# Forming and splitting the feed-forward's gated products in PSUM instead of SBUF

## The chip, the cores and the metric

The kernel runs on one core of a Trainium2 chip. The metric is the device time of one execution in microseconds (us); the median of several runs counts. Engines: TensorE (PE), VectorE (DVE), ScalarE (ACT), GpSimd (POOL), and the DMA queue that SyncE (SP) issues.

## What is computed

Two layers of a hybrid backbone over 512 latent and 256 context tokens of width 1024. Each layer mixes the tokens (Fourier mixing, retention, neighbourhood attention), then applies a gated feed-forward of inner width 2816. The change touches only the feed-forward:

```python
D_FF = ((8 * D_MODEL // 3 + 255) // 256) * 256        # 2816

def swiglu(h, w1, w3, w2):
    return (jax.nn.silu(h @ w1) * (h @ w3)) @ w2

# in each layer
#   x = x + gate * swiglu(rmsnorm(x) modulated, w1, w3, w2)
```

The last layer computes the latent tokens alone.

## The kernel before

**Split operands.** Every matmul operand is kept as two float32r parts: a high part (a ScalarE cast of the fp32 value) and a low part (value minus high part, a subtraction on VectorE or GpSimd). A product is three matmuls: high by high, low by high, high by low (`mm3`, L398 to L400).

**Jobs of seven products.** The products with w1 and w3 are done by Strassen's scheme in Winograd's form. A job is a pair of chunks of 128 output features (r = 0 and 1) for the two halves of the tokens (c = 0 and 1). Its products are issued in the order P1, P2, P6, P7, P4, P5, P3. Each is 12 matmuls of n columns into one PSUM bank, n = 384 in layer 0 and 256 in layer 1. `complete` takes each bank in: P1 is copied to a sum U by ScalarE (L1591); P6 and P7 are added to sums by VectorE (L1595, L1598); P2, P4, P5 and P3 complete the blocks (r, c) = (0, 0), (1, 0), (1, 1) and (0, 1) in `block`. After P5, U also takes the product in for P3 (L1603).

**A block.** For w1, VectorE adds bank and U into the gate tile (L1629) and ScalarE applies SiLU (L1630). For w3, VectorE adds bank and U into a temporary `t` (L1633) and multiplies `t` by the gate into a temporary `g` (L1634); `put` then casts the high part on ScalarE (L1460) and subtracts for the low part (L1461), on VectorE for r = 0 and on GpSimd for r = 1. There are 11 w3 jobs with four blocks in each layer, 44 blocks of n = 384 and 44 of n = 256.

**Parts and the products with w2.** Layer 0 has parts of 2, 1, 2, 2, 2, 2 pairs of jobs (w1, w3), layer 1 of 2, 2, 2, 2, 1, 2. After each part but the last, `plain` multiplies the part's gated products by w2 and VectorE adds the result to the residual x (L1657). The first token half (in layer 0 the first 512 tokens) comes first, for two output chunks together; the gated products of the part's last job come last in each chunk. In this document a handoff is the place where `plain` or `finish` begins to read the part's gated products.

**Weights.** A weight unit arrives by DMA; VectorE forms the sums that Strassen's scheme needs (L225 S, L226, L227, L229); ScalarE casts the high part (L183) and GpSimd, for a few VectorE, subtracts the low part (L188). In layer 0 VectorE also does the next layer's modulation (L522) beside the feed-forward; ScalarE's part of it is L517.

**Order.** The program is scheduled by hand: every engine executes its instructions in the order in which the program writes them, and waits in place. PSUM has eight banks of 512 fp32 columns (`ps`), given out in the order in which they come free; a bank is free when its last reader is done. The first part of each layer begins differently: P1 and P2 of all its four jobs are issued together, beside the layer norm, so that four banks hold P2 until the job's P6 has come. The text calls this the start of a layer's feed-forward.

Of the kernel before, what the change touches and what calls it, by code (L numbers as in the profile page):

```python
# [27 lines left out]
# feed-forward: pairs of chunks between two returns to the residual stream, by layer  # L28
# [5 lines left out]
# for each layer, where the parts of the attentions lie beside the projections: times after the ends of some;  # L34
# the four heads' retention, the readout, the three pairs' of heads neighbourhoods, the first values
# [5 lines left out]
# steps of the operands' preparation beside the first products  # L41
PREP = (0, 1, 1, 2), (1, 1, 1, 2)
# products of the two-by-two scheme in the order of their use
# half of the latent tokens, in the order of the columns, whose mirror images are the others
# [5 lines left out]
# columns of the vector blob  # L50
V_C, V_BADA, V_GMIX, V_GFFN, V_GFIN, V_RETG, V_DEC, V_SEL, V_RP, V_END = 0, 16, 112, 128, 144, 152, 158, 174, 176, 178
# columns of the constant blob
C_ID, C_BLK, C_END = 0, 128, 256
# columns of the decay strips: latent tiles, edge tile, context-context, context-latent
# [4 lines left out]
class Job:  # L59
    """a pair of chunks of outputs, from pairs of chunks of inputs and for two halves of the tokens, by seven  # L60
    products (Strassen's scheme in Winograd's form):
    P1 = A11 B11, P2 = A12 B21, P3 = S4 B22, P4 = A22 T4, P5 = S1 T1, P6 = S2 T2, P7 = S3 T3,
    S1 = A21 + A22, S2 = S1 - A11, S3 = A11 - A21, S4 = A12 - S2,
    T1 = B12 - B11, T2 = B22 - T1, T3 = B22 - B12, T4 = B21 - T2;
    C11 = P1 + P2, C12 = P1 + P6 + P5 + P3, C22 = P1 + P6 + P7 + P5, C21 = P1 + P6 + P7 + P4"""

# [6 lines left out]
def in_order(jobs, after, window):  # L73
    """the order of the jobs' steps on the tensor engine: the oldest job's first step whose operands are there;
    after[key, step]: pairs of another step and a delay"""
    end, t, out = {}, 0.0, []
# [25 lines left out]
class WeightStream:  # L102
    """DMA of the weights in the order of their use, running ahead, and their split into two float32r parts."""

    SLOTS = 11
    # the units of a job that the weights of a product are made from
    USES = {1: (0,), 2: (0,), 3: (0,), 4: (1,), 5: (), 6: (0, 1), 7: (0, 1)}

    def __init__(self, kern, raws, parts):
        self.k = kern  # L110
        self.max_raws, self.max_parts = raws, parts
        self.units, self.tasks = [], []
        self.raw, self.parts, self.size, self.pending = {}, {}, {}, []
        self.when = {}
        self.n_dma = self.n_split = self.n_raw = self.n_parts = 0
        self.limit = 10**6
        # products whose weights' second parts are the vector engine's, of the first jobs and the others
        self.lead, self.dve = {}, {}
        # parts that may go to other places, and those that are there
        self.spare, self.away = 0, set()  # L120
# [5 lines left out]
    def add_step(self, job, p, aps):  # L126
        """the weights of one product of a job, from the two units of its outputs"""
# [8 lines left out]
    def issue(self):  # L136
        """start loads while there is room"""
        k = self.k
# [27 lines left out]
    def part(self, n):  # L166
        """tiles for the two parts of n columns"""
# [23 lines left out]
    def split(self):  # L191
        """split the next unit, or put it aside for its callback"""
# [18 lines left out]
    def form(self, job, p):  # L211
        """the sums that the weights of product p are made from, and those after it"""
# [9 lines left out]
        if p == 6:  # L222
            # S2 takes the place of A11, S3 that of A21 and S4 that of A12
# [49 lines left out]
    def get(self, key):  # L273
        """the parts of a unit, to be followed by done() after its last use"""
        self.flush()
        self.pump()
        return self.parts.pop(key)
# [7 lines left out]
def beside(first, second, kern):  # L285
    """Run two generators side by side; each yields the tensor-engine time of what it has just emitted,
    which kern.pe adds up. The second also yields spans (from, to, cost): its next work lies between these
    times of the first."""
# [22 lines left out]
def pieces(st):  # L311
    """the latent and the context tokens of a stream: which, columns of all tokens, columns of the stream"""
# [7 lines left out]
class Norm:  # L320
    """a layer norm done step by step: the sums, the rows' factors, then a chunk at a time"""
# [28 lines left out]
class Kern:  # L350
# [10 lines left out]
    # ---- tiles  # L361
    def table(self, key, ap):
        """a table of 1024 columns, loaded ahead of its use"""
# [30 lines left out]
    # ---- products of split operands  # L394
    def mm3(self, out, a, b, start, stop):
        """out += a^T b for a = (hi, lo), b = (hi, lo) without the product of the two low parts"""
# [9 lines left out]
    # ---- set-up  # L406
# [18 lines left out]
    def decay_logs(self):  # L425
        """log_sigmoid of the decay logits: min(x, 0) - 2 atanh(z), z = e / (2 + e), e = exp(-|x|)"""
# [21 lines left out]
    # ---- adaLN modulation  # L448
    def ada_load(self, k):
        """weights of the first layer's first shift and scale for the features 8 p + k"""  # L450
# [9 lines left out]
    def ada_first(self, k):  # L460
        """the two's modulation of the features 8 p + k: four groups of columns of the tensor engine share
        the sums, the rows of one stream are then added and turned to partitions"""
# [39 lines left out]
    def ada_unit(self, layer, part, i):  # L502
        """a unit of the first layer's parts in use before its feed-forward, for the tensor engine;
        of the others, for the vector engine"""
# [7 lines left out]
    def silu_tables(self):  # L512
        """silu of the two conditions on all partitions"""
# [5 lines left out]
    def ada_dve(self, raw, layer, part, i):  # L519
        """modulation of the features 8 p + i: a row's products with the condition, summed"""  # L520
# [69 lines left out]
    # ---- layer norm with modulation  # L590
    def sumsq(self, x, m, acc, st):
        """add the squares of chunk m of the residual stream to the sums of acc, those of the last chunk beside them"""
# [8 lines left out]
    def rstd(self, acc, n, merge=True):  # L601
        """1 / RMS of the n tokens, on all partitions of a bank: roots and reciprocals are taken with
        the tokens on partitions"""
# [18 lines left out]
    def modulate(self, x, rs, st, layer, f, h):  # L622
        """h = x rstd g (1 + sc) + sh, split; a generator over the chunks"""
# [37 lines left out]
    # ---- projections  # L661
    def proj(self, key, h, streams, evac):
        """features on partitions: a chunk of 128 columns of the weight against the streams"""
# [18 lines left out]
    def proj_v(self, keys, h, out, norms=None, late=1, heads=False):  # L682
        """tokens on partitions: 384 columns of the weight for the six token tiles;
        with norms the latent tiles come first, beside the layer norms of the two streams"""
# [27 lines left out]
        if heads:  # L712
            # for each token tile the heads' parts side by side, the second of two heads with its low part first
# [17 lines left out]
    def evac_rope(self, dst, tab):  # L731
        """rotary embedding of the latent tokens; the pairs lie 16 partitions apart"""
# [18 lines left out]
    # ---- retention  # L751
    def strip_piece(self, layer, h, piece, delta, st):
        """decay factors of one piece of the strips, an engine's work at a time: delta holds its distances,
        st takes them"""
# [4 lines left out]
        if piece == "cx":  # L759
            # from the context's state in either direction  # L760
# [13 lines left out]
        # both directions have the diagonal  # L774
# [9 lines left out]
    def pieces(self, work):  # L784
        """strip pieces (layer, head, piece, delta, st), a step behind one another"""
# [16 lines left out]
    def strips_first(self):  # L802
        """the first layer's strips: the first head's stay, the others' go to DRAM"""
# [3 lines left out]
        # the distances  # L807
# [43 lines left out]
    def strips_ahead(self, layer, heads):  # L851
        """strips of a later layer, kept in DRAM"""
# [1393 lines left out]
```

## Time and profile before

| what | value |
|---|---|
| runs of the kernel | 1754.65, 1755.63, 1760.47 us, median 1755.63 |
| span of the profiled execution | 1759.0 us |
| PE busy | 1655.9 us, 94% of the span |
| DVE busy | 1219.6 us, 69% |
| POOL busy | 867.1 us, 49% |
| ACT busy | 744.6 us, 42% |
| mean granted TensorE clock | 0.978 |

The profile is of one execution, from its first to its last instruction; no separate time of that execution is listed, so its span stands for it. Busy times add up the durations of an engine's instructions. The layer-0 feed-forward lies between about 480 and 1000 us, that of layer 1 between about 1370 and 1759 us.

### The profile page before, as it was taken

What the parts mean: (1) busy time and instruction counts of PE and PEld (TensorE: products, weight loads), DVE (VectorE), ACT (ScalarE), POOL (GpSimd) and SP (SyncE); (2) the same over time, 40 slices, a digit from 0 to 9 for tenths busy, and PEclk for the clock granted to TensorE, in tenths of its full rate; (3) what the DMA queues carried; (4) which work ended last, traced back from release to release, by engine and by line L of the source; (5) the groups of instructions that cost most, each with busy time, mean ns of one, the idle gap of its engine ahead of it and who ended that gap; (6) DMA issues with size and microseconds to landing.
All of it is one profiled execution on the core that took longest, in us unless ns stands there. A gap on an engine that the chain in (4) does not pass through costs nothing. (4 is left out here: it accounts for less than half of the span.)

```text
span 1759.0 us, 26982 instructions
## 1 busy us (share of the span) xinstructions
PE 1655.9 (94%) x10054; PEld 1481.4 (84%) x10054; DVE 1219.6 (69%) x2040; ACT 744.6 (42%) x1437; POOL 867.1 (49%) x621
## 2 busy tenths in 40 slices
PE   6989999999979998999999999999998799999997
PEld 4867777778978987798999997778788799999997
DVE  6866555664687899586776867764656877767585
ACT  5544434454453223232332554444554444334333
POOL 3343231022467557465665833532035787677673
PEclk9999999999989999999999999999999899999998
DMA  9354243244122343434343444422132232332222
GB/s 344 131 193 133 71 148 94 91 135 167 37 72 85 110 142 108 132 120 132 124 153 114 135 164 138 141 71 87 61 120 73 66 103 87 95 109 84 64 94 72
DMA packets 76387, 202.33 MB, mean 115 GB/s; under 512 B 12704, under 2 KB 19488, under 8 KB 75872
## 3 DMA queue, kind: packets, MB, share of 16 engines
q1 hardware_dynamic: 76256, 200.60, 35.0%
q8 instruction: 80, 1.31, 0.3%
q14 instruction: 51, 0.42, 0.1%
HBM read 184.25 MB, written 11.80 MB: 111 GB/s over the span
## 5 line engine op out<-in xcount | busy, mean ns | idle before, releaser
L188 POOL TENSOR_TENSOR wp<-wr,wp 128x512 fp32r<-128x512 f32 (+1 forms) x336 | 477.5, 1433 | 275.4 <-ACT wp L183 271.8
L399 PE MATMUL f<-hp,wp 128*128 128x384 f32 (+1 forms) x1232 | 387.7, 315 | 13.9 <-POOL wp L188 7.6
L398 PE MATMUL f<-hp,wp 128*128 128x384 f32 (+1 forms) x1232 | 386.9, 314 | 14.5 <-DVE U L1598 5.3
L400 PE MATMUL f<-hp,wp 128*128 128x384 f32 (+1 forms) x1232 | 386.0, 313 | 3.9 <-POOL hp L1523 3.5
L183 ACT CAST wp<-wr 128x512 fp32r<-128x512 f32 (+1 forms) x360 | 213.0, 607 | 355.1 <-PE f L400 117.0
L188 POOL TENSOR_TENSOR wl<-wr,wh 128x1024 fp32r<-128x1024 f32 (+2 forms) x75 | 163.7, 2187 | 379.4 <-ACT wh L183 251.1
L399 PEld LDWEIGHTS f<-hp,wp 128*128 128x128 f32 x1232 | 238.3, 193 | 19.6 <-POOL wp L188 12.9
L398 PEld LDWEIGHTS f<-hp,wp 128*128 128x128 f32 x1232 | 238.6, 194 | 17.8 <-issue 9.7
L400 PEld LDWEIGHTS f<-hp,wp 128*128 128x128 f32 x1232 | 238.4, 194 | 5.2 <-POOL hp L1523 4.3
L398 PE MATMUL f<-g,wp 128*128 128x256 f32 (+1 forms) x576 | 183.6, 319 | 12.8 <-ACT g L1460 12.6
L400 PE MATMUL f<-g,wp 128*128 128x256 f32 (+1 forms) x576 | 183.3, 318 | 4.8 <-POOL g L1461 4.2
L399 PE MATMUL f<-g,wp 128*128 128x256 f32 (+1 forms) x576 | 182.4, 317 | 0.0
L398 PE MATMUL proj<-h,wh 128*128 128x512 f32 (+1 forms) x456 | 167.7, 368 | 0.9 <-DVE v L404 0.9
L399 PE MATMUL proj<-h,wl 128*128 128x512 f32 (+1 forms) x456 | 159.4, 350 | 0.7 <-POOL wl L188 0.7
L400 PE MATMUL proj<-h,wh 128*128 128x512 f32 (+1 forms) x456 | 159.1, 349 | 0.0
L1657 DVE SCALAR_TENSOR_TENSOR x<-f,mod,x 128x256 f32<-128x256 f32 (+1 forms) x160 | 83.8, 546 | 82.8 <-PE f L400 82.7
L398 PEld LDWEIGHTS f<-g,wp 128*128 128x128 f32 x576 | 113.2, 197 | 21.8 <-ACT g L1460 15.2
L400 PEld LDWEIGHTS f<-g,wp 128*128 128x128 f32 x576 | 113.0, 196 | 13.6 <-POOL g L1461 4.8
L399 PEld LDWEIGHTS f<-g,wp 128*128 128x128 f32 x576 | 113.4, 197 | 6.0
L522 DVE CUSTOM_DVE_ANT_0 adj<-wr,tab 128x1024 bf16<-128x1024 f32 x64 | 105.9, 1672 | 10.6 <-DMA wr<-in_w_adat_dram 10.6
L398 PEld LDWEIGHTS proj<-h,wh 128*128 128x128 f32 x456 | 86.6, 190 | 28.6 <-issue 8.3
L399 PEld LDWEIGHTS proj<-h,wl 128*128 128x128 f32 x456 | 86.9, 190 | 11.8 <-POOL wl L188 1.1
(251 smaller groups left out, 3510.1 us busy)
## 6 DMA issues: line engine op xcount, KB each, us to landing
wr<-in_w_dram SPq DMA_DIRECT2D x88, 512.0 KB
wr<-in_w_adat_dram SPq DMA_DIRECT2D x48, 512.0 KB
wr<-in_w_dram SPq DMA_DIRECT2D x80, 256.0 KB
wr<-in_w_ada_dram SPq DMA_DIRECT2D x32, 512.0 KB
ada<-in_w_ada_dram SPq DMA_DIRECT2D x16, 512.0 KB
wr<-in_w_out_dram SPq DMA_DIRECT2D x16, 512.0 KB
tab<-in_rpb_dram SPq DMA_DIRECT2D x12, 512.0 KB
strip<-strips SPq DMA_DIRECT2D x3, 1152.0 KB
```

What stands on the lines that cost most here:

```text
L183: nc.scalar.copy(hi, src)
L188: (nc.vector if vector else nc.gpsimd).tensor_sub(lo, src, hi.bitcast(F32))
L398: mm(out, a[0], b[0], start=start, stop=False)
L399: mm(out, a[1], b[0], start=False, stop=False)
L400: mm(out, a[0], b[1], start=False, stop=stop)
L522: self.nc.vector.tensor_tensor_reduce(out=self.tmp(mybir.dt.bfloat16, D, "adj"), in0=raw, in1=self.tabs[("silu", s)], scale=1.0, scalar=0. ...
L1657: k.nc.vector.scalar_tensor_tensor(xs, ps[:, :n], k.mod[:, self.layer, 5, s, m : m + 1], xs, op0=OP.mult, op1=OP.add)
```

## The change

For w3 blocks, the sum and the product with the gate are written back into the PSUM bank of the matmuls, and the two temporaries `t` and `g` go away. `put` then reads the bank: the ScalarE cast and the subtraction take their source from PSUM. The subtraction is on VectorE for all blocks. Since the bank is now overwritten, the addition of P5 to U[2] moves ahead of the block that P5 completes, for w1 jobs as well. The rest of the diff takes comments and docstrings out; no line number changes.

```diff
         elif p == 5:
+            add(u[2], u[2], ps)
             self.block(job, 1, 1, ps, u.pop(3))
-            add(u[2], u[2], ps)
...
-        t, g = (k.tmp(name="gu")[:, :n] for _ in range(2))
-        nc.vector.tensor_add(t, ps, u)
-        nc.vector.tensor_mul(g, t, gate)
+
+        nc.vector.tensor_add(ps, ps, u)
+        nc.vector.tensor_mul(ps, ps, gate)
         if c == 1:
             del self.gates[q, i, r]
-        self.put([self.chunk(q, self.parts[q][1] * r + i, p)[:, sl] for p in range(2)], g, r == 1)
+        self.put([self.chunk(q, self.parts[q][1] * r + i, p)[:, sl] for p in range(2)], ps, False)
```

## Rows read from the trace of the kernel before

**Rows 1.** Busy us (x instructions) of PE, PEld, DVE, ACT, POOL; PEclk, DMA, GB/s

```profile
510.00:1000.00 490.00, 469.34 (x2628) 439.21 (x2627) 379.31 (x529) 164.00 (x306) 304.51 (x213) 0.99 0.38 123
1385.00:1729.00 344.00, 325.44 (x2600) 321.64 (x2598) 246.44 (x402) 140.54 (x298) 243.52 (x190) 0.97 0.29 90
1450.00:1500.00 50.00, 47.07 (x378) 46.66 (x377) 37.27 (x57) 21.44 (x47) 36.62 (x29) 0.97 0.31 96
```

**Rows 2.** Waits of PE, layer 0 from 490 us: total us, times, longest

```profile
PE f L398 <- ACT g L1460: 8.2, 5, 4.1
PE f L399 <- POOL wp L188: 7.2, 11, 1.1
```

**Rows 3.** Waits of PE, layer 1 from 1370 us

```profile
PE f L398 <- ACT g L1460: 4.4, 3, 1.5
PE f L400 <- POOL g L1461: 4.2, 3, 1.4
PE res L398 <- DVE U L1595: 1.8, 1, 1.8
```

**Rows 4.** Groups by line and form: busy us, mean ns, idle before and its releaser

```profile
L1634 DVE TENSOR_TENSOR gu<-gu,gate 128x384 f32<-128x384 f32 x44 | 44.9, 1020 | 4.1 <-ACT gate L1630 1.8
L1634 DVE TENSOR_TENSOR gu<-gu,gate 128x256 f32<-128x256 f32 x44 | 36.6, 832 | 2.7 <-ACT gate L1630 0.3
L1633 DVE TENSOR_TENSOR gu<-f,U 128x384 f32<-128x384 f32 x44 | 24.3, 552 | 11.4 <-ACT U L1591 7.0 <-PE f L400 2.7 <-DVE U L1598 0.5
L1461 POOL TENSOR_TENSOR g<-gu,g 128x384 fp32r<-128x384 f32 x22 | 30.5, 1386 | 6.3 <-ACT g L1460 6.3
L1461 POOL TENSOR_TENSOR g<-gu,g 128x256 fp32r<-128x256 f32 x22 | 19.8, 905 | 9.6 <-ACT g L1460 9.6
L1461 DVE TENSOR_TENSOR g<-gu,g 128x384 fp32r<-128x384 f32 x22 | 19.5, 887 | 14.1 <-ACT g L1460 14.1
L1461 DVE TENSOR_TENSOR g<-gu,g 128x256 fp32r<-128x256 f32 x22 | 18.9, 860 | 11.7 <-ACT g L1460 11.7
L1633 DVE TENSOR_TENSOR gu<-f,U 128x256 f32<-128x256 f32 x44 | 18.5, 421 | 17.4 <-ACT U L1591 12.9 <-PE f L400 2.5
```

**Rows 5.** Durations of two lines, ns min/median/max

```profile
L1633 DVE TENSOR_TENSOR gu<-f,U x88: 409/484/559, 512.5 to 1727.3; 128x384 f32<-128x384 f32 x44, 128x256 f32<-128x256 f32 x44
L1634 DVE TENSOR_TENSOR gu<-gu,gate x88: 424/1006/1662, 513.0 to 1727.8; 128x384 f32<-128x384 f32 x44, 128x256 f32<-128x256 f32 x44
```

**Rows 6.** DVE in order of time in layer 1: start us, us

```profile
1459.86 1.27 DVE L1634 TENSOR_TENSOR gu<-gu,gate 128x256 f32<-128x256 f32 x1
1462.89 1.18 DVE L1634 TENSOR_TENSOR gu<-gu,gate 128x256 f32<-128x256 f32 x1
1464.78 1.42 DVE L1461 TENSOR_TENSOR g<-gu,g 128x256 fp32r<-128x256 f32 x1 [0.71 <-ACT g L1460]
1466.12 1.78 DVE L225 TENSOR_TENSOR S<-wr 128x512 f32<-128x512 f32 x1
```

**Rows 7.** PE at the handoff near 1486 us

```profile
1485.90 0.39 PE L398 MATMUL f<-g,wp 128*128 128x256 f32 x1 [1.53 <-ACT g L1460]
1487.80 0.39 PE L400 MATMUL f<-g,wp 128*128 128x256 f32 x1 [1.40 <-POOL g L1461]
```

**Rows 8.** ACT ahead of that handoff

```profile
1484.92 0.62 ACT L183 CAST wp<-wr 128x512 fp32r<-128x512 f32 x1 [1.49 <-DMA wr<-in_w_dram]
1485.44 0.71 ACT L1460 CAST g<-gu 128x256 fp32r<-128x256 f32 x2
```

**Rows 9.** POOL at that handoff

```profile
1486.84 1.82 POOL L1461 TENSOR_TENSOR g<-gu,g 128x256 fp32r<-128x256 f32 x2
```

**Rows 10.** DVE ahead of a handoff in layer 0

```profile
804.65 2.06 DVE L522 CUSTOM_DVE_ANT_0 adj<-wr,tab 128x1024 bf16<-128x1024 f32 x1 [0.69 <-DMA wr<-in_w_adat_dram]
```

**Rows 11.** PE at the start of layer 1's feed-forward

```profile
1387.15 0.36 PE L398 MATMUL f<-hp,wp 128*128 128x256 f32 x1 [0.51 <-DVE gu L1633]
```

**Rows 12.** ACT at the start of layer 0's feed-forward

```profile
525.65 1.99 ACT L517 ACTIVATE tab<-tab 128x1024 f32<-128x1024 f32 x2
```

## The prediction

> **What bounds the kernel now.** I read the busy times by stretch first. In layer 0's feed-forward TensorE is busy for 469.34 of 490 us, in layer 1's for 325.44 of 344 us, while DVE has 379.31 and 246.44 us and POOL 304.51 and 243.52 us [rows 1]. So TensorE sets the end, and nothing in this change takes a matmul away: it can give back at most TensorE's idle time there, 20.7 + 18.6 = 39.3 us, and what the lower clock behind an idle stretch costs. [...]
>
> Second came TensorE's waits. In layer 0 it waits 8.2 us for the high parts of gated products (ACT L1460), in five places, and 7.2 us in eleven for low parts of weights (POOL L188) [rows 2]. In layer 1 it waits 4.4 us for the high and 4.2 us for the low parts of gated products, three times each, and 1.8 us for a bank that P6's addition holds [rows 3]. The three in layer 1 are one pattern at three handoffs; the first has 1.53 and 1.40 us [rows 7]. The reader should see there that the wait named GpSimd is one for an instruction that the change takes off GpSimd.
>
> Third, the groups by form, for prices. VectorE's multiplication of two SBUF operands takes 1020 ns for n = 384 and 832 ns for n = 256; the addition just ahead of it, of the same size but with one operand in PSUM, takes 552 and 421 ns [rows 4]. The ranges say why: the addition stays within 409 to 559 ns, the multiplication runs from 424 to 1662 [rows 5]. At its shortest it costs what the addition costs; the rest is time in which GpSimd works on SBUF as well.
>
> **The change part by part.**
>
> *The multiplication with PSUM operands.* No row before has VectorE writing PSUM. From below I take the addition's 552 and 421 ns, since one operand comes from PSUM in both; from above today's 1020 and 832. I take the lower: the pair of operands is what tells the steady line from the stretched one. Saved: 44 x (1.020 - 0.552) + 44 x (0.832 - 0.421) = 38.7 us of VectorE [rows 4].
>
> *The low parts that VectorE has already* (r = 0) go the same way: 22 x (0.887 - 0.552) + 22 x (0.860 - 0.421) = 17.0 us saved [rows 4].
>
> *The low parts that come from GpSimd* (r = 1): GpSimd loses 30.5 + 19.8 = 50.3 us. VectorE gets 22 x 0.552 + 22 x 0.421 = 21.4 us, and a wait with each: it stands idle for the cast in front of its own subtractions, 14.1 / 22 = 0.64 and 11.7 / 22 = 0.53 us each today, so 25.8 us more [rows 4].
>
> VectorE's account is then -38.7 - 17.0 + 21.4 + 25.8 = -8.5 us in 88 blocks: almost nothing. What the change alters is the order of events, so I went to the places where TensorE waits.
>
> [...]
>
> *Handoffs of layer 1 (three).* Now: ACT is held by a weight cast that waits for a DMA until 1484.92, then casts the two gated products; GpSimd takes their low parts at 1486.84, behind weights, and needs 1.82 us for two [rows 8, 9]. TensorE waits 1.53 + 1.40 us [rows 7]. After: VectorE subtracts right behind the cast, at about 1485.44 + 0.36 = 1485.8 to 1486.2, where GpSimd ended the first at 1486.84 + 0.91 = 1487.75: 1.5 us earlier. Against that, P5's and P3's blocks now stand behind that subtraction: 0.42 for U, two additions, two multiplications, a wait and a subtraction more, and half a microsecond for a cast, about 3.5 us, so P3's high part is there at 1489.7. TensorE needs it 18 matmuls after the first low part, at 47.07 / 378 = 0.125 us each 2.2 us after 1487.8, at 1490.0 today [rows 1, 7]. The next wait thus allows 0.3 us. More comes from further ahead: in the pair of jobs before, the blocks' multiplications of 1.27 and 1.18 us and the subtraction of 1.42 become 0.42 each, 2.6 us, against two added subtractions with waits of 0.95, 1.9 us; with the shorter wait of that subtraction (0.71 to 0.53) the weight sums of L225 begin 0.9 us sooner [rows 6], and with them weights, DMA and casts. Bounds: 0.3 us, and the whole 2.93 us; I take 1.6, 4.8 us for the three. [...]
>
> *End of layer 1.* The same shift frees P6's bank earlier by 0.9 us, and the faster P2 block in front of it by another 0.4 + 0.4 or more; 1.8 us of wait [rows 3] go. Bounds 0 to 1.8; I take 1.8.
>
> *Handoffs of layer 0.* VectorE is behind here because of the modulation: L522 takes 2.06 us, after a wait of 0.69 for its DMA [rows 10], and P3's block stands behind it. The DMA does not come earlier, so only L522's stretch and a few tenths of the multiplication go. I take 2.0 of the 8.2 us [rows 2]; bounds 0 and 4.
>
> *Weights in layer 0.* GpSimd's 30.5 us fewer [rows 4] bring some weight parts forward. Of the 7.2 us [rows 2] I take 1.5; bounds 0 and 4.
>
> *The start of each feed-forward.* Here it costs. TensorE already waits for the bank of a w3 block's P2 to be read by L1633, 0.51 us [rows 11]. Now that bank is held through multiplication, cast and subtraction, 0.42 + 0.53 + 0.42 = 1.4 us more, and a later bank wait takes most of that in; I put 0.5 us. In layer 0 the cast of P4's block stands behind two activations of the modulation, 1.99 us [rows 12]; VectorE used to go on with the next blocks meanwhile, and now waits in front of the subtraction, and behind it wait the gates of w1's P5, ACT's SiLU, and the next job's weight sums. I put 2.0 us. Together 2.5 lost; bounds 0 and 5.
>
> *P5's addition to U ahead of its block* costs the block one addition, 0.42 to 0.55 us, and gives it to U: within the lines above. The two temporaries free buffers that no row shows anyone waiting for: nothing.
>
> **Sum.** -4.8 - 1.8 - 2.0 - 1.5 + 2.5 = -7.6 us. The profiled execution's span is 1759.0 us, 3.4 us over the median of the runs; from the one, 1751.4 in a profile, from the other 1755.6 - 7.6 = 1748.0 us.
>
> **The rivals.** *The waits stay (given back).* TensorE's waits at the handoffs come from ACT's queue, held by weights, and from L522; the subtraction only moves from one late engine to another that is in order too. For it: VectorE's account is near zero, and ACT's hold is at 1484.92 whatever VectorE does [rows 8]. Against it: the low part named GpSimd three times [rows 3]. Gains of 0.3 x 3 + 1.8 + 1.0 + 0.5 less 2.5 are 1.7 us: 1754. [...]
>
> *VectorE's wait for the cast gets long (slower).* Each of 44 more subtractions holds VectorE until ACT comes to the cast. At 0.59 us (25.8 / 44) VectorE gains 8.5 us; it loses from 0.59 + 8.5 / 44 = 0.78 us on. At 1.5 us, which is under the 1.99 us of [rows 12], each of nine handoffs and starts has two such blocks, 9 x 2 x 0.9 = 16 us later, and 1764 us comes out. For it: ACT's casts of weights wait for other engines in front of gated casts [rows 8]. Against it: that happens at handoffs, and the mean wait of today's 44 subtractions is 0.59.
>
> [...]
>
> **Numbers.** A measurement here tells 0.3%, 5.3 us, from no change. Forecast 0.43, more than forecast 0.15, given back 0.27, slower 0.15. Of the forecast's own spread (1744 to 1752) about a tenth of all falls within 5.3 us, and of the slower rival a part too: faster 0.53, within 0.34, slower 0.13. Range 1739 to 1758.5: it leaves out the far ends of the first and last, 2 in 10 together.
>
> **What would show it.** Right: no GpSimd line at L1461 for gated products; L1634 and L1461 at 0.42 and 0.55 us, unstretched; the low-part waits of [rows 3] gone, P3's high part the next wait; L225 about 0.9 us sooner behind a w3 job. Wrong: L1634 still over 0.8 us (PSUM writes are dear), idle in front of L1461 over 0.78 us in the mean, or longer bank waits at the starts. The prediction fails most easily if a wait that I traced in one place is replaced by another a microsecond on.

## The result and the profile after

| | before | after |
|---|---|---|
| median of 4 runs each on one chip, us | 1756.76 | 1735.66 |
| lowest to highest, us | 1754.65 to 1760.47 | 1732.88 to 1740.42 |
| span of the profiled execution, us | 1759.0 | 1731.1 |
| mean granted TensorE clock | 0.978 | 0.985 |

The ratio after to before is 0.9871, with a 95% interval from 0.9852 to 0.9890: 21.1 us faster by the medians. The forecast was 7.6 us, and the range ended at 1739.

TensorE runs the same 10054 matmuls in the same order in both kernels, so each matmul of after can be set beside the one of the same number of before. By that, the two profiled executions are 3.3 us apart ahead of any feed-forward; layer 0's feed-forward is 9.3 us shorter (from the start of its first product to the start of its last matmul with w2: 546.3 instead of 555.6), layer 1's 15.3 us shorter (382.0 instead of 397.3), and the stretch between them is unchanged (325.2 and 325.0). The 3.3 us are none of the change's. The 24.6 us in the feed-forwards come from one execution of each kernel and are a little above the 21.1 us of the medians, whose runs lie 6 to 8 us apart (the one of the kernel after is the fastest of its four); lengths of stretches below are of one execution each, and differences under about 2 us are not read.

Busy times by stretch, each covering one feed-forward with a few us around it, and one handoff of layer 1; the columns are those of [rows 1]. First the kernel before, in three stretches that the prediction did not use:

```profile
470.00:1026.00 556.00, 525.79 (x2934) 491.00 (x2933) 438.78 (x611) 201.22 (x380) 346.33 (x242) 0.98 0.36 115
1351.00:1749.00 398.00, 369.99 (x2926) 364.95 (x2925) 290.32 (x477) 168.04 (x361) 271.58 (x215) 0.96 0.26 81
1483.00:1492.00 9.00, 6.07 (x37) 5.66 (x36) 5.28 (x10) 3.82 (x10) 6.83 (x6) 0.82 0.56 195
```

The same stretches of the work in the kernel after:

```profile
466.00:1014.00 548.00, 523.79 (x2942) 492.31 (x2941) 418.46 (x635) 201.94 (x383) 314.97 (x221) 0.98 0.36 116
1338.00:1721.00 383.00, 363.03 (x2928) 358.60 (x2926) 270.90 (x499) 166.66 (x362) 247.72 (x193) 0.98 0.28 84
1467.00:1476.00 9.00, 8.66 (x70) 8.29 (x70) 4.42 (x11) 3.78 (x9) 4.46 (x4) 1.00 0.11 31
```

In layer 1 TensorE's idle time falls from 28.0 to 20.0 us, and its busy time for the same matmuls from 370.0 to 363.0: about half of what is gained there is matmuls that run at a higher granted clock (0.98 instead of 0.96). The 9 us of one handoff show where: 70 matmuls instead of 37, at 1.00 instead of 0.82. Before, the granted clock was 0.50 for 3.4 us behind the waits of each of the three handoffs (from 1488.7, 1557.0 and 1625.2 us); after, it was 1.00 throughout from 1470 to 1690 us.

TensorE's waits after, layer 1 (as [rows 3]; total us, times, longest):

```profile
PE f L398 <- DVE g L1461: 2.7, 2, 1.8
PE res L398 <- DVE g L1461: 2.7, 2, 1.6
...
PE res L398 <- ACT g L1460: 1.5, 1, 1.5
...
PE f L398 <- ACT g L1460: 0.9, 3, 0.3
...
PE f L398 <- DVE U L1598: 0.5, 1, 0.5
```

and layer 0 (as [rows 2]):

```profile
PE f L398 <- ACT g L1460: 4.9, 2, 3.2
PE f L399 <- POOL wp L188: 4.4, 6, 0.9
```

In layer 1 the wait for GpSimd's low parts is gone, and the three waits for high parts are 0.9 us together where they were 4.4 [rows 3]. In their place stand waits for banks that the subtraction L1461 now holds.

The groups by line and form after (as [rows 4]):

```profile
L522 DVE CUSTOM_DVE_ANT_0 adj<-wr,tab 128x1024 bf16<-128x1024 f32 x64 | 101.8, 1608 | 4.0 <-DMA wr<-in_w_adat_dram 3.8
L1634 DVE TENSOR_TENSOR f<-f,gate 128x384 f32<-128x384 f32 x44 | 24.9, 566 | 2.2
L1633 DVE TENSOR_TENSOR f<-f,U 128x384 f32<-128x384 f32 x44 | 24.6, 560 | 11.3 <-ACT U L1591 6.2 <-PE f L400 4.7
L1461 DVE TENSOR_TENSOR g<-f,g 128x384 fp32r<-128x384 f32 x44 | 24.5, 558 | 29.3 <-ACT g L1460 29.3
L1634 DVE TENSOR_TENSOR f<-f,gate 128x256 f32<-128x256 f32 x44 | 19.0, 432 | 1.7
L1461 DVE TENSOR_TENSOR g<-f,g 128x256 fp32r<-128x256 f32 x44 | 18.7, 425 | 33.1 <-ACT g L1460 33.1
```

All three operations of a block now cost the same, 0.43 us for n = 256 and 0.56 for n = 384. VectorE's account: multiplications 81.5 to 43.9 us (-37.6), low parts 38.4 to 43.2 (+4.8), idle for the cast in front of them 25.8 to 62.4 (+36.6) [rows 4]. That is +3.8 us on VectorE, and the kernel is 21 us faster.

### The profile page after: what moved, and what is told of

Its sections match the earlier page's. It is cut to its first block, busy times and chain, and to the rows that moved or that the text cites. A ratio compares the mean times of both kernels' runs of the same rounds, so it can differ in the third digit from the quotient of the medians.

```text
span 1731.1 us, 26920 instructions
## 1 busy us (share of the span) xinstructions
PE 1642.9 (95%) x10054; PEld 1472.8 (85%) x10054; DVE 1179.7 (68%) x2084; ACT 742.5 (43%) x1437; POOL 811.4 (47%) x577
## 3 DMA queue, kind: packets, MB, share of 16 engines
q8 instruction: 80, 1.31, 0.3%
## 5 line engine op out<-in xcount | busy, mean ns | idle before, releaser
L188 POOL TENSOR_TENSOR wp<-wr,wp 128x512 fp32r<-128x512 f32 (+1 forms) x336 | 469.0, 1408 | 312.2 <-ACT wp L183 306.7
L398 PE MATMUL f<-hp,wp 128*128 128x384 f32 (+1 forms) x1232 | 386.5, 314 | 14.1 <-ACT wp L183 3.9
L399 PE MATMUL f<-hp,wp 128*128 128x384 f32 (+1 forms) x1232 | 387.1, 314 | 10.6 <-DVE wp L188 6.2
L188 POOL TENSOR_TENSOR wl<-wr,wh 128x1024 fp32r<-128x1024 f32 (+2 forms) x75 | 163.6, 2186 | 377.9 <-ACT wh L183 282.9
L398 PEld LDWEIGHTS f<-hp,wp 128*128 128x128 f32 x1232 | 237.9, 193 | 17.8 <-issue 6.0
L398 PE MATMUL f<-g,wp 128*128 128x256 f32 (+1 forms) x576 | 180.4, 313 | 5.8 <-ACT g L1460 5.8
L400 PE MATMUL f<-g,wp 128*128 128x256 f32 (+1 forms) x576 | 180.2, 313 | 0.0
L399 PE MATMUL f<-g,wp 128*128 128x256 f32 (+1 forms) x576 | 180.0, 312 | 0.0
L398 PE MATMUL proj<-h,wh 128*128 128x512 f32 (+1 forms) x456 | 167.6, 368 | 0.9 <-DVE v L404 0.9
L398 PEld LDWEIGHTS f<-g,wp 128*128 128x128 f32 x576 | 110.4, 192 | 13.4 <-ACT g L1460 7.2
L400 PEld LDWEIGHTS f<-g,wp 128*128 128x128 f32 x576 | 110.3, 192 | 7.3 <-DVE g L1461 1.1
L399 PEld LDWEIGHTS f<-g,wp 128*128 128x128 f32 x576 | 110.4, 192 | 6.1
L398 PEld LDWEIGHTS proj<-h,wh 128*128 128x128 f32 x456 | 86.6, 190 | 28.7 <-issue 7.4
L522 DVE CUSTOM_DVE_ANT_0 adj<-wr,tab 128x1024 bf16<-128x1024 f32 x64 | 101.8, 1608 | 4.0 <-DMA wr<-in_w_adat_dram 3.8
```

Source lines behind the costliest of these rows:

```text
L188: (nc.vector if vector else nc.gpsimd).tensor_sub(lo, src, hi.bitcast(F32))
L398: mm(out, a[0], b[0], start=start, stop=False)
L399: mm(out, a[1], b[0], start=False, stop=False)
L400: mm(out, a[0], b[1], start=False, stop=stop)
L522: self.nc.vector.tensor_tensor_reduce(out=self.tmp(mybir.dt.bfloat16, D, "adj"), in0=raw, in1=self.tabs[("silu", s)], scale=1.0, scalar=0. ...
```

## The experiments

The result left two readings. **Theory V**: the gain is VectorE's, from a multiplication that no longer has two operands in SBUF. **Theory G**: the gain is GpSimd's, whose 44 subtractions (50.3 us) went away, which the prediction priced only at the handoffs and at 1.5 us of weights. All twelve kernels are given here as the edit to the kernel before, unless said otherwise. Each ratio is to runs of the kernel before that were timed together with it, so ratios can be compared between rows and medians can't. "L0" and "L1" are the lengths of the two feed-forwards in one profiled execution, "handoff" is the mean over those three handoffs of layer 1 at which TensorE waits [rows 3] of the time that the first 30 matmuls from the first one with w2 take.

| kernel | median us | ratio [95%] | L0 | L1 | handoff |
|---|---|---|---|---|---|
| before (profile) | | | 555.6 | 397.3 | 8.1 |
| after | 1735.66 | 0.9871 [0.9852, 0.9890] | 546.3 | 382.0 | 4.1 |
| e1 low parts on VectorE | 1777.68 | 1.0112 [1.0095, 1.0128] | 570.2 | 400.7 | 7.9 |
| e2 multiplication from PSUM | 1736.30 | 0.9876 [0.9857, 0.9894] | 545.7 | 385.9 | 5.6 |
| e3 e2 and low parts on VectorE | 1746.76 | 0.9933 [0.9915, 0.9952] | 551.0 | 390.2 | 5.6 |
| e4 the change, r = 1 on GpSimd | 1733.22 | 0.9854 [0.9834, 0.9873] | 543.3 | 383.4 | 4.6 |
| e5 e2 and a steady extra operation | 1746.31 | 0.9930 [0.9916, 0.9944] | 553.9 | 385.8 | 4.9 |
| e6 low parts from PSUM, multiplication from SBUF | 1755.64 | 0.9976 [0.9965, 0.9987] | 555.9 | 393.9 | 6.1 |
| e7 P5's order alone | 1763.92 | 1.0020 [1.0008, 1.0033] | 556.4 | 400.6 | 8.6 |
| e8 e4, but last jobs on VectorE | 1736.93 | 0.9871 [0.9856, 0.9885] | 545.8 | 382.5 | 4.1 |
| e9 e2 and a stretched extra operation | 1777.68 | 1.0105 [1.0087, 1.0123] | 567.9 | 401.4 | 8.9 |
| e10 e2 in each part's last jobs alone | 1748.97 | 0.9942 [0.9927, 0.9958] | 550.2 | 394.9 | 7.8 |
| e11 e2 in all other jobs alone | 1746.59 | 0.9927 [0.9911, 0.9943] | 549.1 | 389.5 | 5.9 |
| e12 the change, weights back to GpSimd | 1734.61 | 0.9855 [0.9834, 0.9876] | 545.7 | 382.7 | 4.5 |

### e1 to e4: the change's parts one by one

**e1**: all low parts on VectorE, everything else as before.

```diff
-        self.put([...], g, r == 1)
+        self.put([...], g, False)
```

> The kernel before, with one edit: all low parts of gated products on VectorE, sources still in SBUF. Theory G (the gain comes from GpSimd, whose queue loses 44 subtractions, 50 us, in front of the weights' low parts): most of the change's 21 us comes with it, ratio 0.990 to 0.993. Theory V (it comes from VectorE, whose multiplications and subtractions with PSUM sources are no longer stretched by GpSimd): VectorE gets 44 x 0.87 us and 44 waits of 0.59 more, some 64 us, and saves nothing of its own but some stretching; the weight sums of L225 come later, ratio 1.003 to 1.010.

It is 1.12% slower, a little beyond theory V's range. GpSimd lost all of its 44 subtractions of gated products, and whatever that gave was less than what VectorE lost by taking them; so for SBUF sources the gain does not come from moving them. e4 below tries it for PSUM sources. The groups of e1:

```profile
L1634 DVE TENSOR_TENSOR gu<-gu,gate 128x384 f32<-128x384 f32 x44 | 39.3, 893 | 2.3
L1461 DVE TENSOR_TENSOR g<-gu,g 128x384 fp32r<-128x384 f32 x44 | 34.4, 781 | 27.6 <-ACT g L1460 27.6
L1461 DVE TENSOR_TENSOR g<-gu,g 128x256 fp32r<-128x256 f32 x44 | 27.7, 629 | 26.7 <-ACT g L1460 26.7
```

Even without the subtractions GpSimd's other work stretches VectorE's operations with two SBUF operands: 0.78 and 0.63 us where the PSUM source after takes 0.56 and 0.43.

**e2**: only the multiplication's first operand moves; its result and the split stay in SBUF, GpSimd keeps r = 1.

```diff
+            add(u[2], u[2], ps)
             self.block(job, 1, 1, ps, u.pop(3))
-            add(u[2], u[2], ps)
...
-        t, g = (k.tmp(name="gu")[:, :n] for _ in range(2))
-        nc.vector.tensor_add(t, ps, u)
-        nc.vector.tensor_mul(g, t, gate)
+        g = self.k.tmp(name="gu")[:, :n]
+        nc.vector.tensor_add(ps, ps, u)
+        nc.vector.tensor_mul(g, ps, gate)
```

> The change with the product written to an SBUF temporary again and the low parts as before (r = 0 on VectorE, r = 1 on GpSimd, SBUF sources): only the sum in PSUM and the multiplication that reads it remain. Theory V: VectorE saves 38.7 us in 88 multiplications, more than half of the gain: ratio 0.990 to 0.993. Theory G: GpSimd keeps its 50 us, so little: 0.997 to 1.0. The low-part wait for GpSimd at the three handoffs of layer 1 (1.4 us each) should stay by both.

0.9876: the change's whole gain, with none of its moves of the low parts, and more than theory V had allowed for (0.990 to 0.993). Groups of e2:

```profile
L1635 DVE TENSOR_TENSOR gu<-f,gate 128x384 f32<-128x384 f32 x44 | 24.5, 557 | 3.8 <-ACT gate L1630 1.3
L1635 DVE TENSOR_TENSOR gu<-f,gate 128x256 f32<-128x256 f32 x44 | 18.7, 424 | 2.2
L1461 POOL TENSOR_TENSOR g<-gu,g 128x384 fp32r<-128x384 f32 x22 | 24.8, 1127 | 3.1 <-ACT g L1460 3.1
```

The multiplication is at the price that the prediction took. GpSimd's own subtraction gets faster too, 1386 [rows 4] to 1127 ns, though nobody touched it: the two engines had been in each other's way. TensorE's waits of e2 in layer 1 still have the one for GpSimd that the prediction set out to remove:

```profile
PE f L400 <- POOL g L1461: 4.2, 3, 1.4
```

It is as long as before [rows 3], in a kernel as fast as the change.

**e3**: e2, and the low parts of both r on VectorE with the SBUF source (`put(..., g, False)`).

> As the run before, but all low parts on VectorE from the SBUF temporary: it differs from the change only in that the cast and the subtraction read SBUF, and the bank is free after the multiplication. Theory G: nearly the whole gain, 0.987 to 0.990. Theory V: the subtractions are stretched again (0.87 for 0.49 us, 44 x 0.38 x 2 = 33 us of VectorE back): about half, 0.992 to 0.996. At the start of the feed-forwards the waits for banks held by w3 blocks should be as short as before the change (0.5 us in place of 1.75 at the first of layer 1).

0.9933, in theory V's range, so moving 44 SBUF subtractions to VectorE costs 0.57% beside e2, about 10 us.

**e4**: the change, but r = 1 goes by an SBUF temporary to GpSimd as before.

```diff
+        nc.vector.tensor_add(ps, ps, u)
+        g = self.k.tmp(name="gu")[:, :n] if r == 1 else ps
+        nc.vector.tensor_mul(g, ps, gate)
...
+        self.put([...], g, r == 1)
```

> The change for r = 0 alone: the blocks of r = 1 write their product to an SBUF temporary and GpSimd subtracts, as before; all multiplications read PSUM and the low parts of r = 0 are read from PSUM. VectorE saves 38.7 + 17.0 = 55.7 us and gets no wait for a cast in 44 blocks. Theory V: as much as the change or more, 0.985 to 0.989. Theory G: 0.995 to 1.0, GpSimd keeps its 50 us. The low-part wait for GpSimd at layer 1's handoffs stays unless the whole chain ahead comes earlier.

0.9854, an interval that overlaps the change's. Whether 44 of the subtractions stand on VectorE (PSUM source) or on GpSimd does not show in the time, and theory G falls here too: what GpSimd's relief gives and what VectorE's added work and waits cost come to nothing together. The price of the wait for GpSimd is seen to be small here as well; the lines of e4 in layer 1:

```profile
PE f L400 <- POOL g L1461: 2.1, 3, 0.7
...
PE res L400 <- POOL g L1461: 1.7, 1, 1.7
```

### e6 and e7: the other half, and the order alone

**e6**: the converse of e2. The addition goes to SBUF, so the multiplication still reads two SBUF operands; it writes the bank, and cast and subtraction read the bank, all on VectorE (with P5's order).

```diff
+        t = self.k.tmp(name="gu")[:, :n]
+        nc.vector.tensor_add(t, ps, u)
+        nc.vector.tensor_mul(ps, t, gate)
...
+        self.put([...], ps, False)
```

> The change without its part that e2 had alone: the sum goes to an SBUF temporary, the multiplication reads it and the gate from SBUF and writes the bank; cast and low parts as in the change, all on VectorE from PSUM. Theory V: VectorE saves 17.0 us and gets 21.4 + 25.8, plus 30 us more than before, while GpSimd loses 50 us: slower than before or the same, ratio 1.000 to 1.010. If the two parts simply add (change 0.987, e2 0.988), 0.997 to 1.002.

0.9976, a gain of 0.24%, a fifth of the change's. Its multiplication, by the groups:

```profile
L1635 DVE TENSOR_TENSOR f<-gu,gate 128x384 f32<-128x384 f32 x44 | 42.5, 965 | 2.2
L1635 DVE TENSOR_TENSOR f<-gu,gate 128x256 f32<-128x256 f32 x44 | 36.3, 825 | 1.7
```

For the multiplication's duration it is the operand that decides, not where the result goes: 424 and 557 ns into SBUF in e2, 825 and 965 into PSUM here.

**e7**: only P5's addition to U ahead of the block.

> The kernel before with P5 added to U ahead of the block that P5 completes, nothing else. All theories: 0.998 to 1.002. It is in e2 to e4 and in the change as well, and was costed at nothing.

1.0020, [1.0008, 1.0033]: 3.5 us slower. The prediction had costed this at nothing.

### e5 and e9: VectorE's time, or two SBUF operands

Both add to e2 one multiplication per block whose result nobody reads. **e5** takes it from the bank, **e9** from U, so that both its operands are in SBUF. Each run has one of the two marked lines.

```diff
         nc.vector.tensor_add(ps, ps, u)
+        nc.vector.tensor_mul(self.k.tmp(name="junk")[:, :n], ps, gate)   # e5
+        nc.vector.tensor_mul(self.k.tmp(name="junk")[:, :n], u, gate)    # e9
         nc.vector.tensor_mul(g, ps, gate)
```

> The run e2 (only the multiplication reads PSUM) with one more VectorE multiplication in each of the 88 blocks, of PSUM by gate into a temporary that nobody reads, ahead of the real one: some 0.4 us a block, 37 us, about what e2 saved (38.7), at a steady duration that GpSimd does not stretch. Theory V-time (what counts is how long VectorE needs from the sum to the next work in its queue): e2's gain goes, ratio 0.997 to 1.003. Theory V-port (what counts is that two SBUF operands no longer stand against GpSimd, which then is faster as well): most of it stays, 0.987 to 0.991.

> The run e5 with one difference: the idle extra multiplication takes U and gate, two SBUF operands, in place of PSUM and gate. Same count, same place. If the time of VectorE is all that counts, its stretching (0.83 to 1.02 us for 0.42 to 0.56) adds 38 us of VectorE at e5's own price, 10 us for some 37: 1756 us, ratio 0.997 to 1.000. If the port counts on its own, GpSimd and the weights behind it are held up too: 1.002 to 1.010, and L188's mean goes back from 1441 to 1459 ns or over. If two SBUF operands cost nothing beyond their shortest time: 0.993, as e5.

The added operation in e5:

```profile
L1635 DVE TENSOR_TENSOR junk<-f,gate 128x384 f32<-128x384 f32 x44 | 24.5, 558 | 3.4 <-ACT gate L1630 0.9 <-ACT wp L183 0.5
L1635 DVE TENSOR_TENSOR junk<-f,gate 128x256 f32<-128x256 f32 x44 | 18.7, 425 | 1.8
```

and in e9:

```profile
L1635 DVE TENSOR_TENSOR junk<-U,gate 128x384 f32<-128x384 f32 x44 | 45.6, 1037 | 1.0 <-ACT gate L1630 0.9
L1635 DVE TENSOR_TENSOR junk<-U,gate 128x256 f32<-128x256 f32 x44 | 39.3, 893 | 0.0
```

The same instruction on the same engine costs the kernel (0.9930 - 0.9876) x 1759 = 9.5 us with one operand in PSUM, and (1.0105 - 0.9876) x 1759 = 40 us with both in SBUF. It took 558 and 425 ns with one and 1037 and 893 with the other, with GpSimd at work in both. The trace of the kernel before shows the same within one line: of the 44 multiplications of 256 columns, with both operands in SBUF, the 2 during which GpSimd was idle took 425 ns each, and the 18 during which it was busy throughout took 1035 in the mean. The additions just ahead of them, with one operand in PSUM, took 415 ns in the mean where GpSimd was idle (12) and 423 where it was busy throughout (22).

e5 fell between the ranges of its two theories. e9 lies at the far end of the range for two SBUF operands that count on their own, which the expectations call the port (no run shows a port as such), but L188's mean is 1455 ns and not the 1459 or more that this reading asked for.

The two layers differ in what e5's operation costs. In layer 0 the steady operation costs 8.2 us (545.7 to 553.9) for 24.5 us of VectorE's time: there VectorE's time counts, with the modulation's 106 us of L522 in e5 on it. In layer 1 it costs nothing (385.9 and 385.8). Yet additions, extra operations and multiplications of e5 take 18.8 + 18.7 + 18.2 = 55.7 us in layer 1, as much as additions and multiplications before (18.5 + 36.6 = 55.1 [rows 4]), and that feed-forward is 11.5 us shorter than before. VectorE's busy time over that whole stretch is 289.1 us in e5 and 290.3 before. So the total of VectorE's work in layer 1 is not what the gain there is made of. What is left is that a stretched operation comes at a bad place, or holds GpSimd up; these two were not separated. For the place speaks [rows 6]: ahead of a handoff the two multiplications took 1.27 and 1.18 us, not the mean of 0.83. For GpSimd speaks that its subtractions for n = 256 took 905 ns before [rows 4], 785 in e5 and 832 in e9; but its weight parts L188 hardly move (1459, 1441 and 1455 ns in the mean).

### e10 and e11: at the handoffs, or everywhere

e2 with `t = ps` only where the job is a part's last (`i == self.parts[q][1] - 1`), and only where it is not (`i < self.parts[q][1] - 1`); `t` is an SBUF temporary otherwise.

> The multiplication reads PSUM (as in e2) only in the last w3 job of each part, whose gated products TensorE waits for at the handoff; 48 of 88 blocks, the other 40 as before. Theory 'at the handoff' (the gain is made between the last job's products and the w2 products that read them): most of e2's 22 us, ratio 0.988 to 0.992. Theory 'ahead of it' (it comes from the weight sums and DMAs that begin sooner behind the job before): 0.995 to 0.999.

> The converse of e10: the multiplication reads PSUM in all w3 jobs but the last of each part, 40 blocks. Theory 'ahead of the handoff': 0.988 to 0.992; theory 'at the handoff': 0.995 to 0.999. If the two add up to e2, their gains sum to some 22 us.

0.9942 and 0.9927: gains of 0.58 and 0.73%, together 1.31, against 1.24% for e2. Both lie between the ranges of the two theories: neither place has all of it. But the handoffs of layer 1 show something that a look at the handoff alone misses: with fast blocks right ahead of it (e10) it still takes 7.8 us of the 8.1; with fast blocks in the jobs before those (e11) it takes 5.9. The wait at a handoff is made further ahead.

### e8 and e12: looking for a better version

**e8** is e4 with the low parts of each part's last jobs on VectorE (`pool = r == 1 and i < self.parts[q][1] - 1`). **e12** is the change with the 20 low parts of weights that VectorE has in layer 1 given back to the relieved GpSimd:

```diff
-DVE = (({'w1': (7, 4)}, {}), ({'w1': (7, 4)}, {'w1': (7,), 'w3': (4,)}))
+DVE = (({'w1': (7, 4)}, {}), ({'w1': (7, 4)}, {}))
```

> The run e4 (r = 0 in PSUM, r = 1 from an SBUF temporary with the low part on GpSimd), but the last w3 job of each part as in the change, all in PSUM on VectorE. It should keep e4's gain ahead of the handoffs and lose its waits for GpSimd there (three of 0.7 us in layer 1, one of 1.7 at the end): 0.982 to 0.986, 1 to 4 us below e4. If the waits for the cast that the last job gets cost as much, the same as e4.

> The change with one more edit: the low parts of weights that VectorE makes in layer 1 beyond the first jobs (20 of them, two SBUF operands, 1.2 us each) go back to GpSimd, which lost 22 subtractions of gated products there. By the runs so far, each operation of two SBUF operands on VectorE costs it over 1 us and holds GpSimd up: the layer-1 feed-forward should get 2 to 5 us shorter, ratio 0.984 to 0.987, at or below the change and e4. Rival: GpSimd, which paces the weights at layer 1's handoffs (a cast and a subtraction take turns at 2.02 us), becomes the bound: 0.988 to 0.995.

e8 was to beat e4 and did not (0.9871 against 0.9854, intervals that overlap). e12 has 0.9855, in its forecast range, but overlaps the change as well. All of the change, e2, e4, e8 and e12 lie within 0.3% of one another; no version was found that is shown to be faster than the change.

## Why the prediction was wrong

The sign and the first price were right, the size was not: 21.1 us measured, 7.6 forecast. What came is the case "more than forecast", which had a chance of 0.15: at each of layer 1's three handoffs 2.6 of the 2.93 us of waits went, where the sum took 1.6, and 1.5 us of faster matmuls came with them, which the sum leaves out; layer 0's handoffs gained 4.5 us more than forecast. The low end of the range has room for the clock by an estimate with a full speed that no run shows; what the runs showed there is a granted clock of 0.50 for 3.4 us at each of the three handoffs before, and of 1.00 after.

In the terms of the sum, read from the shift of equal-numbered matmuls: handoffs of layer 1 forecast 4.8 us, measured 12.1; handoffs of layer 0 forecast 2.0, measured 6.5; end of layer 1 forecast 1.8, measured 1.9; starts forecast 2.5 lost, measured 1.6 gained. The other 2.5 us of the 24.6 lie between these places, 2.0 of them in layer 0 between its second and third handoff. So the size failed at the handoffs.

**The multiplication.** Right: the lower bound, 432 and 566 ns in place of 832 and 1020, unstretched (431 to 567 ns over 88). Writing PSUM costs VectorE 8 to 9 ns more than writing SBUF (424 and 557 ns in e2). A PSUM source does not show as dearer here: a subtraction of 256 columns from PSUM takes 425 ns, where the shortest multiplication of two SBUF operands before took 424 [rows 5].

**The step that failed is the one from VectorE's account to the handoffs.** The account's terms were nearly right: -38.7 came out as -37.6, -17.0 + 21.4 as +4.8, and the 25.8 of added waits as 36.6. The inference from "almost nothing" to the time was wrong. It put a microsecond of idle in front of a subtraction on a level with a microsecond of a stretched multiplication. e2 has the multiplication's part alone and the whole gain; beside it the low parts' part is worth nothing in time (the change against e2 and e4), though it costs VectorE 36.6 us of idle time; without it that part is worth 0.24% (e6). My reading is that a wait for a cast mostly uses up time in which VectorE would wait for TensorE or ACT a few instructions on anyway. That is not shown: no run takes those waits away alone, GpSimd's relief may have paid for them, and at one handoff of layer 0 the moved subtractions do cost time (below). The stretched operation delays what stands behind it and, as e2's faster GpSimd shows, the engine that it stretches against. Having closed the account at zero, the prediction looked for the gain only at TensorE's waits and sized each from what stands right ahead of it: 4.8 and 2.0 us at the handoffs, where 12.1 and 6.5 were measured.

**Handoffs of layer 1** were 4.8 us and measured 12.1: three times 8.1 to 4.1. Ahead of TensorE at one of them, the kernel after shows:

```profile
1473.58 0.39 PE L398 MATMUL f<-g,wp 128*128 128x256 f32 x1 [0.34 <-ACT g L1460]
```

The next wait is P3's high part, as forecast, and 0.34 us long, as forecast (0.3). But it is the only one. On ACT ahead of it:

```profile
1468.96 0.62 ACT L183 CAST wp<-wr 128x512 fp32r<-128x512 f32 x1 [1.40 <-POOL wp L188]
1469.49 0.36 ACT L1460 CAST g<-f 128x256 fp32r<-128x256 f32 x1
```

The weight cast that held ACT until a DMA came [rows 8] now waits for GpSimd, and ends so early that the first gated cast comes 2.3 us sooner against TensorE's matmuls. "ACT's hold is at 1484.92 whatever VectorE does" was the mistaken sentence. The DMA was not even the pattern of the three handoffs: at the second and third the same cast already waited for GpSimd before the change, as here at the second:

```profile
1553.13 0.62 ACT L183 CAST wp<-wr 128x512 fp32r<-128x512 f32 x1 [1.39 <-POOL wp L188]
```

What held ACT there is a chain of weight casts and GpSimd's subtractions behind one another, and VectorE delays that chain in two places. One is a stretched multiplication: before the change, the weight cast that starts 2.6 us ahead of the first matmul with w2 stands right behind a gated cast that waits for such a multiplication. That gated cast before and after:

```profile
1480.22 0.41 ACT L1460 CAST g<-gu 128x256 fp32r<-128x256 f32 x1 [1.33 <-DVE gu L1634]
```

```profile
1463.00 0.37 ACT L1460 CAST g<-f 128x256 fp32r<-128x256 f32 x1 [0.45 <-DVE f L1634]
```

The other is the weight sums. On VectorE, after:

```profile
1450.73 0.68 DVE L225 TENSOR_TENSOR S<-wr 128x512 f32<-128x512 f32 x1
```

This is the weight sum that the prediction had 0.9 us sooner; it starts 18.75 us ahead of the first handoff's first matmul where it was 17.0, so 1.75 us sooner. The weight cast that waits for these sums, before and after, starts 13.7 and 15.5 us ahead of that matmul:

```profile
1469.45 0.62 ACT L183 CAST wp<-wr 128x512 fp32r<-128x512 f32 x1 [3.92 <-DVE wr L227]
```

```profile
1453.94 0.62 ACT L183 CAST wp<-wr 128x512 fp32r<-128x512 f32 x1 [2.79 <-DVE wr L227]
```

The next load moves with the sums too. In all kernels but e12 it is issued 3.3 us behind the end of L229; it goes out 9.6 us ahead of that matmul before, and 11.5 after:

```profile
1473.51 0.33 SPq L145 DMA_DIRECT2D wr<-in_w_dram  x1
```

```profile
1458.00 0.33 SPq L145 DMA_DIRECT2D wr<-in_w_dram  x1
```

Over all fourteen kernels an early sum goes with a short handoff: the eight that start it 18.3 us or more ahead take 4.1 to 5.9 us, the six with 17.0 or less take 6.1 to 8.9. Within the two groups the order does not hold, and no run moves the sums alone. e11 agrees with it: the jobs further ahead decide.

The clock, which the sum leaves out, is the rest: of the 4.1 us that a handoff became shorter, 2.6 were waits (1.53 + 1.40 [rows 7] less 0.34) and 1.5 faster matmuls.

**Handoffs of layer 0** were 2.0 us and measured 6.5, unevenly: the five gained 1.4, -3.0, 1.9, 4.6 and 1.6 us. At the second, behind the part with one pair of jobs, TensorE waits longer for the high part than before (0.23 us there):

```profile
614.32 0.50 PE L398 MATMUL f<-g,wp 128*128 128x512 f32 x1 [1.72 <-ACT g L1460]
```

The runs show why. The six kernels in which VectorE makes all low parts of a part's last job (the change, e1, e3, e6, e8, e12) wait 1.7 to 2.3 us there; the six that leave r = 1 to GpSimd and add no operation (before, e2, e4, e7, e10, e11) wait 0 to 0.3. So here the moved subtractions and their waits for casts do cost TensorE time, as the account had it. At the fourth, "the DMA does not come earlier" was the wrong sentence. L522's wait for its DMA fell from 10.6 us in all to 4.0 (the first row of the groups after), and the one that had 0.69 [rows 10] starts 2.9 us sooner against TensorE's matmuls and takes 1.23 us instead of 2.06:

```profile
795.24 1.23 DVE L522 CUSTOM_DVE_ANT_0 adj<-wr,tab 128x1024 bf16<-128x1024 f32 x1 [0.16 <-DMA wr<-in_w_adat_dram]
```

**Weights in layer 0**: 1.5 forecast; TensorE's waits for them fell by 2.8 (7.2 to 4.4 [rows 2]).

**End of layer 1**: 1.8 forecast, 1.9 measured, and that is luck. The forecast wait for P6's bank, 1.8 us [rows 3], did go, but the waits `PE res L398` listed above, 2.7 and 1.5 us at the same place, took its gain away: over the products with w2 the matmuls do not move. The 1.9 us come from further ahead, where the first matmul of one of the last part's products had waited for VectorE's addition for a gate of w1, and now does not. Before:

```profile
1711.20 0.35 PE L398 MATMUL f<-hp,wp 128*128 128x256 f32 x1 [1.21 <-DVE gate L1629]
```

**The starts** were to lose 2.5 us and lost nothing: from the first product to the first matmul with w2, layer 0 took 83.7 and then 82.9 us, layer 1 68.7 and then 67.9. The first half of the reasoning held. TensorE at the start of layer 1's feed-forward, after:

```profile
1375.54 0.38 PE L398 MATMUL f<-hp,wp 128*128 128x256 f32 x1 [1.75 <-DVE g L1461]
1382.11 0.36 PE L398 MATMUL f<-hp,wp 128*128 128x256 f32 x1 [0.52 <-DVE U L1598]
1386.31 0.38 PE L398 MATMUL f<-hp,wp 128*128 128x256 f32 x1 [0.97 <-DVE g L1461]
```

The bank is held longer, 1.75 us of waiting where it was 0.51 [rows 11], and a new wait of 0.97 comes. But the wait for U between them, before the change

```profile
1395.03 0.36 PE L398 MATMUL f<-hp,wp 128*128 128x256 f32 x1 [2.98 <-DVE U L1598]
```

is 0.52 now: "a later bank wait takes most of that in" was true to the point of taking in all. e3, whose bank is free after the multiplication, shows the same trade the other way:

```profile
1379.55 0.36 PE L398 MATMUL f<-hp,wp 128*128 128x256 f32 x1 [0.22 <-DVE gu L1635]
...
1386.91 0.55 PE L398 MATMUL f<-hp,wp 128*128 128x256 f32 x1 [2.81 <-DVE U L1598]
```

**P5's order** at nothing was wrong by 3.5 us on its own (e7). What it costs inside the change was not measured.

**The slower rival** had the right place. The mean wait for a cast came to 62.4 / 88 = 0.71 us, not far from the 0.78 from which VectorE was to lose; and nothing was lost, because that bound came from the same account.

**What stays open**: in layer 1, how much a stretched operation costs by its own length at a bad place and how much by holding GpSimd; how much of the shorter handoffs is due to the earlier weight sums and how much to ACT's shorter wait for the multiplication; and whether, away from layer 0's second handoff, VectorE's waits for casts are free or paid for by GpSimd's relief.

## What to carry to other kernels

Where a value comes out of a PSUM bank anyway, an elementwise operation with two SBUF operands beside a busy GpSimd can be worth giving that operand in PSUM, even in place: 88 of them at 0.43 and 0.56 us instead of 0.83 and 1.02 brought 1.24% here, and moving GpSimd's subtractions to VectorE as well brought nothing beside it. Don't close an engine's account with busy time and idle time as equals: ask what each microsecond delays, and follow a wait to the jobs ahead of it, along the casts and sums that the weights go through. Where an idle stretch of TensorE ends, count the faster matmuls behind it too: here the granted clock was 0.50 for 3.4 us behind each of three such stretches, and in layer 1 faster matmuls were about half of the gain.

## What the runs showed of the hardware

A VectorE multiplication that writes into the PSUM bank that it reads (L1634 after, 432 and 566 ns) costs nearly what it costs to write SBUF (424 and 557 ns in e2). ScalarE's cast takes less from PSUM than from SBUF: 372 and 479 ns after, 404 and 513 before (L1460). And the stretch works both ways: GpSimd's subtraction of 384 columns went from 1386 to 1127 ns in e2, where of all operands only the first of VectorE's multiplication was moved. It has no fixed price: VectorE's own subtractions of 384 columns, with two SBUF operands in both kernels, took 887 ns before [rows 4] and 1097 in e2.
